# Gates in four parts, block copies in two, and the symmetrised rows of a triangular solve in four strips

## The chip, the cores and the metric

The kernel runs on one core of a Trainium2 chip. The metric is the device time of one execution in microseconds. The kernel before was timed in three runs: 1096.52, 1096.67 and 1097.42 us, a median of 1096.67 us.

Names of engines in the profile: PE is TensorE (matmuls), PEld its weight loads, DVE is VectorE, ACT is ScalarE, POOL is GpSimd, SP is the engine that issues the DMAs here.

## The reference

One layer of a hybrid model on 384 tokens of 1024 channels: 128 context tokens, which start from zero states and use their own conditioning vector, and 256 latent tokens, which start from cached states. The same weights serve both.

```python
x += 0.5 * gate1 * swiglu_1(rmsnorm(x) * (1 + scale1) + shift1)
P  = (rmsnorm(x) * (1 + scale2) + shift2) @ w_in          # 1024 -> 9248
yA = W_a(B * conv3(C * x_a))                              # short gated convolution
yB = W_dn(rmsnorm_head(o_fwd + o_bwd) * silu(z))          # two-way gated DeltaNet, 8 heads of 128
x += gate2 * W_o(sigmoid(g_A) * yA + sigmoid(g_B) * yB)
x += 0.5 * gate3 * swiglu_2(rmsnorm(x) * (1 + scale3) + shift3)
y  = rmsnorm(x)
```

For the DeltaNet, `g = -exp(a_log) * softplus(a_raw + dt_bias)` is a decay for each token, head and direction; chunks of tokens build `T = I + tril(beta * (k k^T) * decay, -1)` and solve a unit triangular system with it. The matrix `T` depends on the keys and gates alone, so it is inverted once for each head, direction and chunk. The outputs are the normalised tokens and the new forward and backward states.

## The kernel before

**Layout and matmuls.** Channels lie on partitions, the 384 tokens along the free axis, as three blocks of 128. Every large product is made in split fp32: a weight unit of 128 × 1024 numbers, loaded by DMA, is rounded by ACT into a high part `hi` (L270), DVE subtracts to get the low part `lo` (L280), and three matmuls of 384 columns (L288, L289, L290: high × high, high × activations' low part, low × high) are accumulated for each of the unit's eight 128 × 128 blocks. So a unit is 24 matmuls, in two **halves** of 12. The third matmul of a unit is the first that reads `lo`. Both parts are made for the unit after next: `hi` is issued behind the first half of a unit, `lo` behind the second.

**Order of the work.** Each engine runs its instructions in the order in which the program writes them. All small work (convolutions, gates, the DeltaNet) is written as Python generators, which the function `gemm` moves forward between its halves by two calls, `tick("V")` and `tick("P")`: each calls every live generator once, if it is in that phase. A pair `yield; yield` in a generator means "go on one half later"; what stands between two such pairs is issued in one piece, on whatever engines it uses. The order of the generators in a gap is: queued evacuations, the DeltaNet, the gates, other evacuations.

**Gates.** `gates` (L655 to L727) makes the decays. It transposes the raw gate columns (`nat`), runs exponentials on ACT (L682, L683), evaluates the softplus by a polynomial of 17 small DVE instructions in one piece (L695 to L710), waits `GLAG[3]` = 4 halves beside a pair of its own, sums the decays with matmuls into `cs`, and exponentiates them into `ex`. The exact sums of `g` are also used by the decay masks of the DeltaNet (L836 to L853).

**Evacuations.** `evac_qkv` takes each head's q, k or v from PSUM: ACT copies it into a padded tile (L797, edges L756 and L757) and makes the middle tap of the convolution (L761), one half later DVE adds the outer taps (L766, L767), one half later again ACT makes a tanh `ct` (L808) and DVE the SiLU `kT`, `qT` or `cy` (L810), some yields later PE transposes the result (L815).

**DeltaNet.** `dn` (L858 to L1224) runs once for each group of four heads; the second group starts when the first sets `free`. It builds the masked matrices `M` (L914), copies their 32 × 32 diagonal blocks into `Md` (L940 to L947: eight copies for two directions, half of them on ACT at L945, half on DVE at L947), all in one gap; one half later DVE transposes the blocks (L951, `Lt`) and adds the transpose (L953) to get the symmetrised rows `L3`, 1024 elements on each partition, and one tick later the solve starts: 31 columns (L996 to L1008), each a product (L1000) and a subtraction (L1002) over `(j+1)·n` elements, where `n = 31 - j`. A running `cost` decides how many columns share a gap: when it exceeds `LCOST[gr]` the generator yields, lets another generator (`fst`, matmuls with the cached states) take a step, and yields again. Summed by that formula, the solve of group 0 (0.7) is cut at 25 places and the one of group 1 (0.9) at 19. After the solve stand two transposes (L1010, L1012) and eight block copies (`diag`, L1027 on ACT and L1029 on DVE), all issued in one piece. The inverse is then completed by matmuls and the outputs normalised (a power on POOL at L1210, L1213 on DVE, twelve scalings on ACT at L1219).

**What runs beside it.** While group 0 is in the solve, PE runs the units of w_in that feed the short convolution (its evacuations are L1314 and L1326). Three pairs of units for the gate and output convolution (`pairs_(0, NP0)`, L1356) stand before the loop at L1357, which would tick without matmuls until `free` is set. Then the k, q and v heads of group 1 and the remaining pairs (evacuation L1347) run beside the second group.

Of the kernel before, what the change touches and what calls it, by code (L numbers as in the profile page):

```python
# [9 lines left out]
ALU = mybir.AluOpType  # L10
# [8 lines left out]
FB = 22  # L19
H = 8  # L20
EPS = 1e-6
LCOST = (0.7, 0.9)
NP0 = 3
LAG = (7, 5, 9)
GLAG = (2, 2, 0, 4)
K1 = 2
NMM = 3
R1 = 4
# [123 lines left out]
def program(nc, tc, a, o, ctx, ExitStack):  # L152
    V, A, G, T = nc.vector, nc.scalar, nc.gpsimd, nc.tensor
    LEFT, RIGHT = "left", "right"

    def bc(ap, *shape):
        return ap.to_broadcast(list(shape))
# [27 lines left out]
    def sbank(name="sd"):  # L185
        return pss.tile([P, 512], F32, tag="sd", name=name)
# [394 lines left out]
    def residual(x, k, out, gates):  # L581
        for c, s0, s1 in SEG:
            V.scalar_tensor_tensor(x[:, k, s0:s1], out[:, s0:s1], gates[:, k, c:c + 1], x[:, k, s0:s1],  # L583
                                   op0=ALU.mult, op1=ALU.add)
# [70 lines left out]
    def gates(hf, wba, gp, tmp, res):  # L655
        def lag(n):
            for _ in range(2 * n):
                yield
        yield from lag(GLAG[0])
        pba = sbank("pba")  # L660
        for k in range(8):
            g = k % 4
            T.matmul(pba[32 * g:32 * g + 32, :NT], wba[:, k, :], hf[:, k, :], start=(k < 4), stop=(k >= 4))
        res["pba"] = pba
        yield
        ba = tmp()
        A.activation(ba, pba[:, :NT], AF.Copy)
        na = gp.tile([P, 16], F32, name="na")
        A.activation(na, W["alog"], AF.Exp)
        V.tensor_scalar(na, na, -1.0, None, op0=ALU.mult)  # L670
        yield
        yield from lag(GLAG[1])
        nat = sbank("nat")
        for b in range(3):
            T.transpose(nat[:, b * P:(b + 1) * P], ba[:, b * P:(b + 1) * P], C["ident"])
        yield
        nv = ba[:, :96].rearrange("p (b c) -> p b c", b=3)
        q, x, e, s, s2, s4, p = (ba[:, i:i + 48] for i in (0, 96, 144, 192, 240, 288, 336))
        V.tensor_reduce(nv, nat[:, :NT].rearrange("p (b g c) -> p b c g", b=3, g=4), axis=AX.X, op=ALU.add)
        V.tensor_tensor(x.rearrange("p (b c) -> p b c", b=3), nv[:, :, 16:32], bc(W["dtb"].unsqueeze(1), P, 3, 16),  # L680
                        op=ALU.add)
        A.activation(e, x, AF.Abs)  # L682
        A.activation(e, e, AF.Exp, scale=-1.0)  # L683
        beta = gp.tile([P, 2, 3, 8], F32, name="beta")
        g = gp.tile([P, 2, 3, 8], F32, name="g")
        A.activation(beta, nv[:, :, 0:16].rearrange("p b (d h) -> p d b h", d=2), AF.Tanh, scale=0.5)
        G.tensor_scalar(beta, beta, 0.5, 0.5, op0=ALU.mult, op1=ALU.add)
        nab = bc(na.unsqueeze(1), P, 3, 16)

        def b16(t):  # L690
            return t.rearrange("p (b c) -> p b c", b=3)
        yield
        yield
        yield from lag(GLAG[2])
        V.tensor_scalar(s, e, 2.0, None, op0=ALU.add)  # L695
        V.reciprocal(s, s)
        V.tensor_tensor(s, s, e, op=ALU.mult)
        V.tensor_tensor(s2, s, s, op=ALU.mult)
        V.scalar_tensor_tensor(b16(x), b16(x), 0.0, nab, op0=ALU.max, op1=ALU.mult)
        V.tensor_tensor(s4, s2, s2, op=ALU.mult)  # L700
        V.scalar_tensor_tensor(b16(s), b16(s), 2.0, nab, op0=ALU.mult, op1=ALU.mult)
        V.tensor_scalar(p, s4, 1.0 / 13, None, op0=ALU.mult)
        V.tensor_scalar(q, s4, 1.0 / 15, None, op0=ALU.mult)
        for n in (9, 5):
            V.scalar_tensor_tensor(p, p, 1.0 / n, s4, op0=ALU.add, op1=ALU.mult)
            V.scalar_tensor_tensor(q, q, 1.0 / (n + 2), s4, op0=ALU.add, op1=ALU.mult)
        V.scalar_tensor_tensor(q, q, 1.0 / 3, s2, op0=ALU.add, op1=ALU.mult)
        V.scalar_tensor_tensor(p, p, 1.0, q, op0=ALU.add, op1=ALU.add)
        V.tensor_tensor(p, p, s, op=ALU.mult)
        V.tensor_tensor(g, p.rearrange("p (b d h) -> p d b h", b=3, d=2),  # L710
                        x.rearrange("p (b d h) -> p d b h", b=3, d=2), op=ALU.add)
        yield
        yield from lag(GLAG[3])
        cs = sbank("cs")
        g2 = g.rearrange("p d b h -> p d (b h)")
        for j, masks in enumerate(((C["le"], C["ge"]), (strict[:, 0].bitcast(F32), strict[:, 1].bitcast(F32)))):
            for d in range(2):
                T.matmul(cs[:, j * 48 + 24 * d:j * 48 + 24 * d + 24], masks[d], g2[:, d], start=True, stop=True)
        T.matmul(cs[:, 96:144], ones, g.rearrange("p d b h -> p (d b h)"), start=True, stop=True)
        yield  # L720
        ex = gp.tile([P, 3, 2, 3, 8], F32, name="ex")
        A.activation(ex.rearrange("p a d b h -> p (a d b h)"), cs[:, :144], AF.Exp)
        gh = gp.tile([P, 2, 3, 8], F32R, name="gh")
        gl = gp.tile([P, 2, 3, 8], F32, name="gl")
        A.activation(gh, g, AF.Copy)
        V.tensor_tensor(gl, g, gh.bitcast(F32), op=ALU.subtract)
        res["beta"], res["gs"], res["ex"] = beta, (gh.bitcast(F32), gl), ex  # L727


    def mixer(x, acc, esb, es, nt, raw, tail_pool, on_wo):  # L730
# [127 lines left out]
        def dn(gr, d, dp, ready):  # L858
# [38 lines left out]
            for b in range(3):  # L897
# [3 lines left out]
                if b == 0:  # L901
                    V.tensor_scalar(n2, d["ssk"], 4.0 * EPS, None, op0=ALU.add)
                    G.tensor_tensor(rk.rearrange("p b h -> p (b h)"), n2.rearrange("p b h -> p (b h)"), phalf[:, :12],
                                    op=ALU.pow)
# [18 lines left out]
            def scores():  # L923

                while not ready("q", 4):
                    yield
                V.tensor_scalar(nq, d["ssq"], 4.0 * EPS, None, op0=ALU.add)
                G.tensor_tensor(rq.rearrange("p b h -> p (b h)"), nq.rearrange("p b h -> p (b h)"), mhalf[:, :12],
                                op=ALU.pow)
                for b in range(3):  # L930
                    kq = sbank("kq")
                    four(kq, lambda h: kT[:, h, b * P:(b + 1) * P], lambda h: qT[:, h, b * P:(b + 1) * P])
                    yield
                    for dd in range(2):
                        V.tensor_tensor(f2(Dm[dd][:, b]), kq, f2(Dm[dd][:, b]), op=ALU.mult)
                    yield
                V.tensor_scalar(rq, rq, float(P) ** -0.5, None, op0=ALU.mult)
            post = scores()

            for dd in range(2):  # L940
                for q in range(4):
                    src = Mn[dd][32 * q:32 * q + 32, :, 32 * q:32 * q + 32]
                    dst = Md[32 * q:32 * q + 32, :, 12 * dd:12 * dd + 12].rearrange("p i n -> p n i")
                    if q % 2 == 0:
                        A.activation(dst, src, AF.Copy)  # L945
                    else:
                        V.tensor_copy(dst, src)  # L947
            yield
            yield
            Lt = dp.tile([P, 32, 32], F32, tag="Lt", name="Lt")  # L950
            V.transpose(Lt, Md)  # L951
            L3 = dp.tile([P, 32, 32], F32, tag="Md", name="L3")
            V.tensor_tensor(L3, Lt, Lt.rearrange("p i j -> p j i"), op=ALU.add)  # L953
            Z3 = Zl
            yield
            egc, edec, egl = (ex[:, i, :, :, h0:h0 + 4] for i in range(3))
# [38 lines left out]
            cost = 0.0  # L995
            for j in range(31):  # L996
                n = 31 - j
                t = dp.tile([P, 256], F32, tag="lt", name="lt")
                t3 = t[:, :(j + 1) * n].rearrange("p (c i) -> p c i", i=n)
                V.tensor_tensor(t3, bc(Z3[:, 0:j + 1, j:j + 1], P, j + 1, n),  # L1000
                                bc(L3[:, j:j + 1, j + 1:32], P, j + 1, n), op=ALU.mult)
                V.tensor_tensor(Z3[:, 0:j + 1, j + 1:32], Z3[:, 0:j + 1, j + 1:32], t3, op=ALU.subtract)  # L1002
                cost += 0.4 + 2.1e-3 * (j + 1) * n
                if cost > LCOST[gr] and j < 30:
                    cost = 0.0
                    yield
                    next(fst, None)
                    yield  # L1008
# [280 lines left out]
        def start(gr):  # L1289
            d = holder["d"]  # L1290
            while "ex" not in res:
                yield
                yield
            spawn(dn_decay(gr, d, dp), now=False)
            yield from dn(gr, d, dp, lambda kinds, n: all(nev.get(k, 0) >= 4 * gr + n for k in kinds))

        gen = spawn(start(0), now=False)
        spawn(gates(hf, wba, gp, lambda: t384("cv"), res), "P", now=False)

        ch = cpl.tile([P, 8, NT], F32R, tag="c0", name="ch")  # L1300
# [443 lines left out]
```

## Time and profile before

| | |
|---|---|
| median of three runs | 1096.67 us |
| the profiled execution | 1097.54 us |
| its span | 1095.8 us |
| mean granted clock of TensorE | 0.994 |
| PE busy | 1076.1 us (98%) |
| DVE busy | 796.7 us (73%) |
| ACT busy | 485.3 us (44%) |
| POOL busy | 119.2 us (11%) |
| gates' polynomial, L695 to L710 | 354.32 to 357.54 us |
| block copies, `Lt` and `L3` of group 0 (DVE) | 2.11, 1.24 and 2.08 us |
| solve of group 0, first column | at 415.76 us |
| solve of group 1, first and last column | at 596.96 and 639.97 us |

A row of a timeline reads: start, duration, engine, line, operation, output <- inputs, partitions × elements, and in brackets the idle time before it and what ended it. Neighbouring instructions of one kind are joined (xN). A row of a table of stretches has, for each engine, the busy time and the count, then the TensorE clock that was granted (1.00 is full speed), the DMA share and the traffic. A row of waits has the total, the number and the longest.

### The profile page before, as it was taken

What the parts mean: (1) busy time and instruction counts of PE and PEld (TensorE: products, weight loads), DVE (VectorE), ACT (ScalarE), POOL (GpSimd) and SP (SyncE); (2) the same over time, 40 slices, a digit from 0 to 9 for tenths busy, and PEclk for the clock granted to TensorE, in tenths of its full rate; (3) what the DMA queues carried; (4) which work ended last, traced back from release to release, by engine and by line L of the source; (5) the groups of instructions that cost most, each with busy time, mean ns of one, the idle gap of its engine ahead of it and who ended that gap; (6) DMA issues with size and microseconds to landing.
All of it is one profiled execution on the core that took longest, in us unless ns stands there. A gap on an engine that the chain in (4) does not pass through costs nothing. (4 is left out here: it accounts for less than half of the span.)

```text
span 1095.8 us, 17468 instructions
## 1 busy us (share of the span) xinstructions
PE 1076.1 (98%) x7031; PEld 1056.8 (96%) x7031; DVE 796.7 (73%) x1367; ACT 485.3 (44%) x907; POOL 119.2 (11%) x102
## 2 busy tenths in 40 slices
PE   9999999999999999999999999999999999999997
PEld 7799999999998999999998999999999999999997
DVE  3799988898879899985599986555669765443442
ACT  3563333322357873352586343343357333333332
POOL 1300000000031441011360111100011000000000
PEclk9999999999999999999999999999999999999999
DMA  9566756666435423332332432336425643333331
GB/s 367 203 244 247 269 209 249 233 233 253 147 121 173 135 78 102 129 116 83 131 109 85 128 132 78 126 115 230 143 89 206 220 182 122 115 131 125 118 128 58
DMA packets 35969, 174.34 MB, mean 159 GB/s; under 512 B 3376, under 2 KB 10288, under 8 KB 22704
## 3 DMA queue, kind: packets, MB, share of 16 engines
q1 hardware_dynamic: 35888, 173.23, 44.3%
q8 instruction: 55, 0.90, 0.3%
q14 instruction: 26, 0.21, 0.1%
HBM read 166.66 MB, written 6.55 MB: 158 GB/s over the span
## 5 line engine op out<-in xcount | busy, mean ns | idle before, releaser
L288 PE MATMUL mm<-hh,hi 128*128 128x384 f32 x1200 | 406.9, 339 | 0.0
L290 PE MATMUL mm<-hh,lo 128*128 128x384 f32 x1200 | 402.7, 336 | 2.3 <-DVE lo L280 2.1
L289 PE MATMUL mm<-hl,hi 128*128 128x384 f32 x1200 | 402.1, 335 | 0.0
L270 ACT ACTIVATE hi<-raw 128x1024 fp32r<-128x1024 f32 (+1 forms) x238 | 242.0, 1019 | 274.3 <-PE mm L289 177.2
L280 DVE TENSOR_TENSOR lo<-raw,hi 128x1024 fp32r<-128x1024 f32 (+1 forms) x238 | 286.0, 1203 | 100.0 <-ACT hi L270 99.8
L290 PEld LDWEIGHTS mm<-hh,lo 128*128 128x128 f32 x1200 | 225.8, 188 | 3.8 <-DVE lo L280 3.8
L288 PEld LDWEIGHTS mm<-hh,hi 128*128 128x128 f32 x1200 | 226.0, 188 | 1.5 <-issue 0.6
L289 PEld LDWEIGHTS mm<-hl,hi 128*128 128x128 f32 x1200 | 225.9, 188 | 0.6 <-DVE hl L555 0.2
L481 DVE SCALAR_TENSOR_TENSOR junk<-adw,cb 128x1024 f32<-128x1024 f32 x112 | 136.6, 1219 | 0.7
L288 PE MATMUL mm<-ah,hi 128*128 128x384 f32 x352 | 117.6, 334 | 0.0
L289 PE MATMUL mm<-al,hi 128*128 128x384 f32 x352 | 117.6, 334 | 0.0
L290 PE MATMUL mm<-ah,lo 128*128 128x384 f32 x352 | 117.6, 334 | 0.0
L288 PEld LDWEIGHTS mm<-ah,hi 128*128 128x128 f32 x352 | 66.1, 188 | 0.0
L289 PEld LDWEIGHTS mm<-al,hi 128*128 128x128 f32 x352 | 66.1, 188 | 0.0
L290 PEld LDWEIGHTS mm<-ah,lo 128*128 128x128 f32 x352 | 66.1, 188 | 0.0
L618 DVE TENSOR_TENSOR gu<-mm,sg 128x384 f32<-128x384 f32 x38 | 21.2, 557 | 35.6 <-PE mm L290 35.6
L442 DVE TENSOR_TENSOR al<-gu,ah 128x384 fp32r<-128x384 f32 x44 | 24.2, 556 | 17.2 <-ACT ah L441 17.2
L575 ACT ACTIVATE sqt<-xT 128x384 f32<-128x384 f32 x20 | 10.5, 525 | 58.1 <-DVE xT L583 58.1
L552 POOL TENSOR_TENSOR xr<-xT,sqacc 128x384 f32<-128x384 f32 x24 | 29.3, 1233 | 28.9 <-DVE h L566 9.7
L746 POOL MEMSET xp<- 128x396 f32 x3 | 1.2, 429 | 251.4 <-DVE al L442 161.0
L1634 POOL TENSOR_TENSOR r<-ms,mhalf 128x1 f32<-128x1 f32 x1 | 0.5, 548 | 255.2 <-DVE ms L1633 255.2
L331 DVE SCALAR_TENSOR_TENSOR xl<-xT,amod,xh 128x128 fp32r<-128x128 f32 (+1 forms) x48 | 27.3, 605 | 1.2 <-ACT xh L321 1.1
(326 smaller groups left out, 1369.3 us busy)
## 6 DMA issues: line engine op xcount, KB each, us to landing
raw<-wts SPq DMA_DIRECT2D x91, 1024.0 KB, 4.9
adw<-adaT SPq DMA_DIRECT2D x28, 1024.0 KB, 7.1
raw<-wts SPq DMA_DIRECT2D x16, 896.0 KB, 4.6
ad<-ada SPq DMA_DIRECT2D x8, 1024.0 KB, 10.5
raw<-wts SPq DMA_DIRECT2D x10, 768.0 KB, 4.4
cb<-condb SPq DMA_DIRECT2D x2, 1024.0 KB, 7.6
raw<-wts SPq DMA_DIRECT2D x4, 384.0 KB, 9.7
xsp<-xT SPq DMA_DIRECT2D x1, 1536.0 KB, 9.7
```

The lines of the kernel that those rows point to most:

```text
L270: A.activation(hi[:, :n], raw, AF.Copy)
L280: V.tensor_tensor(lo[:, :n], raws[c][:, off:off + n], hi[:, :n].bitcast(F32), op=ALU.subtract)
L288: T.matmul(out, wh[:, off:off + width], rh, start=first, stop=False)
L289: T.matmul(out, wh[:, off:off + width], rl, start=False, stop=False)
L290: T.matmul(out, wl[:, off:off + width], rh, start=False, stop=last)
L331: V.scalar_tensor_tensor(xl[:, s0:s1], x[:, k, s0:s1], amod[:, i, k, c:c + 1], xh[:, s0:s1].bitcast(F32), op0=ALU.mult, op1=ALU.subtract)
L442: V.tensor_tensor(lo, x, hi.bitcast(F32), op=ALU.subtract)
L481: V.scalar_tensor_tensor(junk, t[:, s], 1.0, cb[:, c], op0=ALU.mult, op1=ALU.mult, accum_out=modT[:, v, j + s, c:c + 1])
L552: G.tensor_tensor(xs[k], x[:, k, :], rbs, op=ALU.mult)
L575: A.activation(t, x[:, k, :], AF.Square)
L618: V.tensor_tensor(t, pu, sg, op=ALU.mult)
L746: G.memset(t, 0.0)
```

## The change

Four edits, no matmul or DMA is added or removed.

1. The polynomial of the gates is cut into four parts of 4, 5, 4 and 4 instructions, each one half after the part before; `GLAG[3]` goes from 4 to 2.
2. The block copies of the two directions stand in two gaps, one half apart, and begin one half later than before.
3. The add that makes `L3` is cut into four strips of eight rows; each is written ahead of the column that first needs it (0, 8, 16, 24) and only from the strip's second column on: 8 × 31, 8 × 23, 8 × 15 and 8 × 7 elements instead of 1024. The running cost is raised by 0.003·n at each.
4. `LCOST` goes from (0.7, 0.9) to (0.8, 1.0). By the formula the solve of group 0 is then cut at 23 places, the one of group 1 at 15.

```diff
-LCOST = (0.7, 0.9)
+LCOST = (0.8, 1.0)
...
-GLAG = (2, 2, 0, 4)
+GLAG = (2, 2, 0, 2)
...
         V.tensor_tensor(s2, s, s, op=ALU.mult)
+        yield
+        yield
         V.scalar_tensor_tensor(b16(x), b16(x), 0.0, nab, op0=ALU.max, op1=ALU.mult)
...
         V.tensor_scalar(q, s4, 1.0 / 15, None, op0=ALU.mult)
+        yield
+        yield
         for n in (9, 5):
             V.scalar_tensor_tensor(p, p, 1.0 / n, s4, op0=ALU.add, op1=ALU.mult)
             V.scalar_tensor_tensor(q, q, 1.0 / (n + 2), s4, op0=ALU.add, op1=ALU.mult)
+        yield
+        yield
         V.scalar_tensor_tensor(q, q, 1.0 / 3, s2, op0=ALU.add, op1=ALU.mult)
...
             post = scores()
 
+            yield
+            yield
             for dd in range(2):
                 for q in range(4):
...
                     else:
                         V.tensor_copy(dst, src)
-            yield
-            yield
+                yield
+                yield
             Lt = dp.tile([P, 32, 32], F32, tag="Lt", name="Lt")
             V.transpose(Lt, Md)
             L3 = dp.tile([P, 32, 32], F32, tag="Md", name="L3")
-            V.tensor_tensor(L3, Lt, Lt.rearrange("p i j -> p j i"), op=ALU.add)
...
             for j in range(31):
                 n = 31 - j
+                if j % 8 == 0:
+                    V.tensor_tensor(L3[:, j:j + 8, j + 1:32], Lt[:, j:j + 8, j + 1:32],
+                                    Lt[:, j + 1:32, j:j + 8].rearrange("p i j -> p j i"), op=ALU.add)
+                    cost += 0.3e-2 * n
```

## The prediction

> **What bounds the kernel now.** I read the page's busy shares first, then the whole list of waits on TensorE, then each of those waits in the timelines of PE, DVE and ACT.
>
> ```profile
> span 1095.8 us, 17468 instructions
> PE 1076.1 (98%) x7031; PEld 1056.8 (96%) x7031; DVE 796.7 (73%) x1367; ACT 485.3 (44%) x907; POOL 119.2 (11%) x102
> PE mm L290 <- DVE lo L280: 5.2, 4, 2.5
> PE tr L815 <- DVE kT L810: 2.9, 1, 2.9
> ```
>
> TensorE sets the time. It is busy for 1076.1 of 1095.8 us, and in the stretch that the change touches it waits five times: once for `kT` (2.9 us) and four times for the low half of a weight unit, `lo` (5.2 us together). No matmul is added or removed, so the change is worth what it does to these five waits, to the clock after them, and to waits that do not exist yet. The five in PE's timeline:
>
> ```profile
> 354.85 0.34 PE L290 MATMUL mm<-hh,lo 128*128 128x384 f32 x1
> 358.07 0.55 PE L815 MATMUL tr<-cst,kT 128*128 128x128 f32 x3 [2.88 <-DVE kT L810]
> ...
> 418.17 0.34 PE L289 MATMUL mm<-hl,hi 128*128 128x384 f32 x1
> 420.23 0.44 PE L290 MATMUL mm<-hh,lo 128*128 128x384 f32 x1 [1.72 <-DVE lo L280]
> ...
> 543.40 0.44 PE L290 MATMUL mm<-hh,lo 128*128 128x384 f32 x1 [0.41 <-DVE lo L280]
> ...
> 597.79 0.34 PE L289 MATMUL mm<-cl,hi 128*128 128x384 f32 x1
> 600.60 0.45 PE L290 MATMUL mm<-ch,lo 128*128 128x384 f32 x1 [2.48 <-DVE lo L280]
> ...
> 612.01 0.44 PE L290 MATMUL mm<-ch,lo 128*128 128x384 f32 x1 [0.56 <-DVE lo L280]
> ```
>
> Successive matmuls start about 0.17 us apart when nothing stops them, so each wait costs its start-to-start gap less 0.17: 3.05 at 358, 1.89 at 420, about 0.58 at 543, 2.64 at 600.6 and about 0.73 at 612. After two of them the granted clock falls. Columns of the next rows: stretch, length, then busy time and count for PE, PEld, DVE, ACT, POOL, then the granted clock.
>
> ```profile
> 358.07:362.09 4.02, 4.02 (x16) 4.02 (x16) 3.40 (x5) 3.50 (x19) 0.00 (x0) 0.58 0.48 145
> 600.60:604.60 4.00, 4.00 (x15) 3.90 (x16) 3.76 (x11) 2.23 (x4) 0.00 (x0) 0.57 0.74 250
> 569.00:646.00 77.00, 73.97 (x448) 73.10 (x447) 73.70 (x155) 38.23 (x87) 6.76 (x6) 0.98 0.33 109
> ```
>
> At clocks of 0.58 and 0.57 these stretches lose 0.42 × 4.02 = 1.69 and 0.43 × 4.00 = 1.72 us. The last row matters most: over the 77 us of head group 1's preparation and solve, DVE is busy for 73.70. There DVE, not PE, sets the pace.
>
> **The change part by part.** First the gates.
>
> ```profile
> 354.32 0.22 DVE L695 TENSOR_SCALAR cv<-cv 128x48 f32<-128x48 f32 x1
> 355.30 0.21 DVE L698 TENSOR_TENSOR cv<-cv 128x48 f32<-128x48 f32 x1
> 357.33 0.21 DVE L710 TENSOR_TENSOR g<-cv 128x48 f32<-128x48 f32 x1
> 357.46 0.55 DVE L810 SCALAR_TENSOR_TENSOR kT<-ct,cy 128x384 f32<-128x384 f32 x1
> 356.03 0.51 ACT L808 ACTIVATE ct<-cy 128x384 f32<-128x384 f32 x1
> ```
>
> The polynomial's 17 instructions hold DVE from 354.32 to 357.46, and `kT`, which PE transposes next, stands behind them. In four parts only L695 to L698 stay ahead of it, and they end near 355.5. But `kT` also needs `ct` from ACT, whose row ends at 356.54. So `kT` runs 356.6 to 357.15 instead of 357.46 to 358.0, and the transpose starts near 357.2: 0.9 us saved, not 3.05. The other three parts take (357.46 − 355.42) = 2.0 us in later half units; they fit into DVE's waits for `ct`. Without that cover one of them delays a `lo` by at most 0.9 (the largest part). A second gain hangs on the clock: the idle time shrinks from 2.88 to about 2.0, between 1.72 (after which the profile shows no dip) and 2.48 (after which it does). If the dip goes, 1.69 more is saved. I take a dip as 35% likely: 0.9 + 0.65 × 1.69 = **−2.0**; ends −2.6 and 0 (a part in the way of a `lo`). The shorter GLAG nets to one half unit (12 matmuls, 12 × 0.173 = 2.08 us) later for the decay sums and all of group 0 behind them.
>
> [...]
>
> Now head group 0's solve.
>
> ```profile
> 412.01 1.24 DVE L951 STREAM_TRANSPOSE Lt<-Md 128x1024 f32<-128x1024 f32 x1
> 413.28 2.08 DVE L953 TENSOR_TENSOR L<-Lt 128x1024 f32<-128x1024 f32 x1
> 418.95 1.22 DVE L280 TENSOR_TENSOR lo<-raw,hi 128x1024 fp32r<-128x1024 f32 x1
> ```
>
> The wait at 420.23 is for the `lo` at 418.95, behind which stand 1.24 + 2.08 us of one-off work and the 2.11 us of block copies. The change deals the copies into two gaps and the add into strips of 8 × 31, 8 × 23, 8 × 15 and 8 × 7 = 608 of 1024 elements. At the row's 2.08 us per 1024, with 0.17 fixed for each (the shortest rows of the solve, 31 elements, take 0.17 to 0.19), the strips take 4 × 0.17 + 608 × 1.87 ns = 1.81 us, the first 0.63. Rows of plain L1000 products of the same sizes (0.41 for 247 elements, down to 0.22 for 60) would make it 1.3. So it saves 0.27 to 0.8 in all, and 1.45 ahead of column 0. With two halves (4.16 us) more room for copies and transpose, and 1.45 less in the way, the `lo` that was 1.89 late has some 4 us to spare. The wait of 1.89 and a tail of about 0.3 at 426 go: −2.2. The other side: LCOST 0.8 packs the columns of this group into 23 half-unit pairs of ticks instead of 25 (counted by summing 0.4 + 2.1e-3·(j+1)·n, plus 0.3e-2·n at each strip, against the bound), so the middle gaps hold more and one `lo` near 438 comes about 0.7 late. **−1.5**; ends −2.2 and 0.
>
> Group 0's end then comes one half unit later in program order (+1 gates, +2 copies, −2 columns) while it is the same work.
>
> ```profile
> 537.51 3.63 ACT L1219 ACTIVATE on<-on,mo 128x128 f32<-128x128 f32 x12 [5.92 <-DVE mo L1213]
> 542.12 2.36 DVE L280 TENSOR_TENSOR lo<-raw,hi 128x1024 fp32r<-128x1024 f32 x2 [4.71 <-ACT hi L270]
> ```
>
> ACT's twelve L1219 instructions hold up `hi`, `hi` holds up `lo`, and PE loses 0.58 at 543. Moved a half later the same block stands before the first `kT` of group 1 as well; I price that as one more wait of the same size: **+0.5**; ends 0 (it lands where ACT has room) and +1.0 (two more).
>
> Then group 1, where the sign of the whole is decided.
>
> ```profile
> 586.66 3.67 ACT L945 ACTIVATE Md<-M 32x384 f32<-32x384 f32 x4
> 590.35 0.52 ACT L808 ACTIVATE ct<-cy 128x384 f32<-128x384 f32 x1
> 590.90 0.56 DVE L810 SCALAR_TENSOR_TENSOR cy<-ct,cy 128x384 f32<-128x384 f32 x1 [1.09 <-ACT ct L808]
> 593.79 2.07 DVE L953 TENSOR_TENSOR L<-Lt 128x1024 f32<-128x1024 f32 x1
> 599.33 1.22 DVE L280 TENSOR_TENSOR lo<-raw,hi 128x1024 fp32r<-128x1024 f32 x1
> ...
> 636.84 1.22 DVE L280 TENSOR_TENSOR lo<-raw,hi 128x1024 fp32r<-128x1024 f32 x1
> 640.00 1.25 DVE L1010 STREAM_TRANSPOSE O<-Zl 128x1024 f32<-128x1024 f32 x1
> 645.57 1.23 DVE L280 TENSOR_TENSOR lo<-raw,hi 128x1024 fp32r<-128x1024 f32 x1
> ...
> 641.92 0.34 PE L290 MATMUL mm<-ch,lo 128*128 128x384 f32 x1
> 646.98 0.34 PE L290 MATMUL mm<-hh,lo 128*128 128x384 f32 x1
> ```
>
> The wait at 600.6 vanishes where it is: strips and an earlier transpose bring its `lo` forward by 2 to 4 us, and it needs 2.64. But PE then only runs into a queue that has not become shorter. The `lo` that starts at 645.57 ends at 646.80 and its matmul starts at 646.98: after 2.64 + 0.73 + 1.72 = 5.1 us of lost PE time, DVE is just on time. Take away the early wait and the same 5.1 us come back later unless DVE's work shrinks or moves. Four things move it. The strips save 0.27 to 0.8. The one idle time of DVE, 1.09 at 590.9, becomes about 2.4, since ACT's copies (3.67 us for four) are dealt into two gaps and the second pair stands ahead of the `ct` that DVE needs, while less DVE work covers it: +1.3. LCOST 1.0 packs 31 columns into 15 half-unit pairs instead of 19; with the copies' +2 the closing block (L1010 to the last L1029, 640.00 to 645.57) moves two halves, one unit, ahead in program order. So the block must now be done before the `lo` of the unit before, whose matmul stands at 641.92. The new time of that `lo` is the old block's end, 645.57, less the 1.7 us of the old `lo` and the L1347 merge behind it that now come later, plus 1.3 idle, less 0.5 strips, plus 1.2 for itself: about 645.9; bounds 644.6 (no new idle) to 646.4. PE reaches it at 641.92 plus one `kq` of 0.8 us that moves ahead too: 642.7. That is 1.9 to 3.7 more of wait than now; **I take +2.5**, as a little of it falls where the clock is down anyway. Ends: −5.1 (DVE is not the limit after all and the waits simply go) and +5.0 (3.3 plus one more dip of 1.7 behind the last wait).
>
> Sum: −2.0 − 1.5 + 0.5 + 2.5 = **−0.5**. The profiled execution took 1097.54, 0.87 above the median of 1096.67, so 1097.54 − 0.5 − 0.87 = **1096.2 us**.
>
> [...]
>
> **Rivals.** *Faster, group 1's waits break even or go.* For it: PE's idle time of 2.48 and its dip stand at one place, and the change takes the work away from that place; a DVE share of 73.70 in 77.00 still leaves 3.3 us. Against it: the matmul at 646.98 with nothing to spare. If group 1 breaks even, −2.0 − 1.5 + 0.5 = −3.0, 1093.7; if its waits go altogether, −8.1, 1088.6. *Slower, the packed solve of group 1 drops the clock behind its last wait.* Fifteen gaps hold what nineteen held, the closing block stands a unit earlier, and PE waits there in one piece for up to 3.7 us; from some 2.5 us of idle time the clock falls, and at the end of the stage nothing is left that a slower PE could wait for, so 1.7 counts in full: group 1 costs +5.0. With the dip at 358 kept as well (−0.9 there) the sum is −0.9 − 1.5 + 0.5 + 5.0 = +3.1, 1099.8. Against it: the waits may split into short ones, as at 600 and 612 now. *The polynomial's split does nothing*, since `ct` sets `kT`'s start: that alone moves the sum by +0.9 and stays within what can be told apart.
>
> **How the numbers follow.** About 0.2%, 2.2 us, is what a measurement of this kernel can tell from no change. My forecast (−0.5, reaching ±2.2) has 0.40. Group 1 breaking even or better has 0.36, of which 0.12 for its waits going altogether. The slower rival has 0.24. Range: 1089.0 to 1100.3, which leaves out the fullest form of either side; the forecast's own range is 1094.5 to 1098.9. Faster 0.36, same 0.40, slower 0.24.
>
> **What would show it.** Stall 1: the `kT` wait at 355 shorter than 2.88 and naming `ct` behind it, and whether the clock is 1.00 from 358 to 362. Group 0: no `lo` wait near 420, a shorter one near 438. Group 0's end: L1219, `hi` and `lo` around 543 to 550. Group 1: the 600.6 wait gone and new `lo` waits between 605 and 647, DVE's share from 569 to 646 above 0.95 with an idle time at `ct` near 590, and O1 a unit earlier against PE. I am wrong if the sum of `lo` waits in group 1 falls below 3 us with O1 moved ahead: then DVE was not the limit.

## The result, and the profile after

The change makes the kernel slower: 1103.19 us in the median (1101.34 to 1104.3), against 1097.05 us for the kernel before timed beside it, a ratio of 1.0062 (95% interval 1.0050 to 1.0074), or some 6 us. The forecast was 1096.2 with a range up to 1100.3. The profiled execution of the changed kernel took 1101.34 us, so it is the quickest of its four, 1.9 us below their median.

Its page, and the whole list of waits on TensorE in the stretch from 300 to 720 us:

```profile
span 1099.6 us, 17474 instructions
PE 1074.4 (98%) x7031; PEld 1053.3 (96%) x7031; DVE 796.8 (72%) x1373; ACT 483.7 (44%) x907; POOL 120.7 (11%) x102
PE mm L290 <- DVE lo L280: 10.4, 8, 3.0
PE tr L821 <- DVE kT L816: 2.6, 3, 2.0
```

PE's work is what it was, and so is DVE's (796.8 against 796.7). The waits for `kT` are shorter, as forecast, but those for `lo` have doubled, from 5.2 to 10.4 us. (Line numbers move by 6 behind the gates and by 11 from the solve on: L810 is L816, L1000 is L1011.) PE's timeline has them at these places:

```profile
355.46 0.55 PE L821 MATMUL tr<-cst,kT 128*128 128x128 f32 x3 [1.99 <-DVE kT L816]
...
421.67 0.44 PE L290 MATMUL mm<-hh,lo 128*128 128x384 f32 x1 [0.91 <-DVE lo L280]
...
432.31 0.44 PE L290 MATMUL mm<-hh,lo 128*128 128x384 f32 x1 [0.26 <-DVE lo L280]
...
437.47 0.44 PE L290 MATMUL mm<-hh,lo 128*128 128x384 f32 x1 [0.73 <-DVE lo L280]
...
479.08 0.44 PE L290 MATMUL mm<-hh,lo 128*128 128x384 f32 x1 [1.52 <-DVE lo L280]
...
603.08 0.44 PE L290 MATMUL mm<-hh,lo 128*128 128x384 f32 x1 [1.16 <-DVE lo L280]
608.53 0.44 PE L290 MATMUL mm<-ch,lo 128*128 128x384 f32 x1 [0.66 <-DVE lo L280]
616.28 0.44 PE L290 MATMUL mm<-hh,lo 128*128 128x384 f32 x1 [2.98 <-DVE lo L280]
...
646.53 0.44 PE L290 MATMUL mm<-ch,lo 128*128 128x384 f32 x1 [2.21 <-DVE lo L280]
```

To see where time comes from and goes to, I matched the mixer's main matmuls of the two traces in their order and took the difference of their starts, at places where no small PE work stands on different sides. The first is at 333.94 before and 332.23 after. That difference of 1.71 us is older than any changed instruction, so it is taken off.

| same matmul, before | after | after less before, less the start | what lies in the stretch |
|---|---|---|---|
| 333.94 | 332.23 | 0 | |
| 367.71 | 363.49 | −2.51 | gates: shorter wait, no dip of the clock |
| 457.27 | 453.89 | −1.67 | rest of the gates' delay, most of group 0's solve |
| 534.16 | 533.14 | +0.69 | closing block of group 0 |
| 573.65 | 572.95 | +1.01 | group 0's output, first keys of group 1 |
| 741.53 | 745.31 | +5.49 | all of group 1 |

So 2.5 us are won at the gates, 3.5 are lost again by the end of group 0, and 4.5 in group 1. The sum of 5.5 is close to the 6 us of the medians. From here on "by 457", "by 574" and "by 742" mean these differences at the third, fifth and sixth place.

**Group 0's solve.** DVE's rows ahead of the `lo` that PE waits for at 421.67 and, last, POOL's:

```profile
416.61 0.64 DVE L1006 TENSOR_TENSOR L<-Lt 128x248 f32<-128x248 f32 x1
417.28 0.92 DVE L1011 TENSOR_TENSOR lt<-Zl,L 128x31 f32<-128x31 f32 x1
418.23 0.97 DVE L1013 TENSOR_TENSOR Zl<-Zl,lt 128x31 f32<-128x31 f32 x1
419.23 0.99 DVE L1011 TENSOR_TENSOR lt<-Zl,L 128x60 f32<-128x60 f32 x1
420.26 0.22 DVE L1013 TENSOR_TENSOR Zl<-Zl,lt 128x60 f32<-128x60 f32 x1
420.40 1.22 DVE L280 TENSOR_TENSOR lo<-raw,hi 128x1024 fp32r<-128x1024 f32 x1
416.61 3.54 POOL L994 TENSOR_TENSOR vn<-vn,rk 128x512 f32<-128x512 f32 x3 [17.62 <-ACT vn L825]
```

While POOL multiplies `vn`, the first three rows of the solve take 0.92 to 0.99 instead of about 0.2 us, 2.2 us more ahead of that `lo`. In the kernel before POOL starts this work at 421.71, behind the wait at 420. The four strips themselves take 0.64, 0.49, 0.38 and 0.25, together 1.76 (forecast 1.81).

**Group 0's closing block.** ACT's rows and one of DVE's, of the changed kernel:

```profile
472.14 1.84 ACT L1038 ACTIVATE XP<-O 32x384 f32<-32x384 f32 x2 [6.81 <-DVE O L1023]
473.99 1.81 ACT L1038 ACTIVATE M<-O 32x384 f32<-32x384 f32 x2
475.83 1.06 ACT L270 ACTIVATE hi<-raw 128x1024 fp32r<-128x1024 f32 x1
476.80 0.51 ACT L441 ACTIVATE ch<-cv 128x384 fp32r<-128x384 f32 x1
477.21 0.47 ACT L1316 ACTIVATE xp<-mm 128x384 f32<-128x384 f32 x1
477.58 1.04 ACT L270 ACTIVATE hi<-raw 128x1024 fp32r<-128x1024 f32 x1
477.81 1.22 DVE L280 TENSOR_TENSOR lo<-raw,hi 128x1024 fp32r<-128x1024 f32 x1
```

Four block copies hold ACT for 3.65 us. Behind them stand `hi` and `ch`, and the `lo` that PE waits for at 479.08 stands on DVE behind the instruction that needs `ch` (L442, which waits 2.78). The kernel before has the same ACT rows at nearly the same times and the same `lo` at 477.85, but there PE comes to the matmul that needs it only at 481.37 and doesn't wait.

**Group 1's packed gap.** DVE's rows and, last, POOL's:

```profile
611.05 0.40 DVE L1011 TENSOR_TENSOR lt<-Zl,L 128x231 f32<-128x231 f32 x1
611.48 1.28 DVE L1013 TENSOR_TENSOR Zl<-Zl,lt 128x231 f32<-128x231 f32 x1
612.80 1.13 DVE L1011 TENSOR_TENSOR lt<-Zl,L 128x240 f32<-128x240 f32 x1
613.97 1.13 DVE L1013 TENSOR_TENSOR Zl<-Zl,lt 128x240 f32<-128x240 f32 x1
615.01 1.21 DVE L280 TENSOR_TENSOR lo<-raw,hi 128x1024 fp32r<-128x1024 f32 x1
611.47 3.36 POOL L994 TENSOR_TENSOR vn<-vn,rk 128x512 f32<-128x512 f32 x3 [36.88 <-DVE lt L1011]
```

While POOL multiplies `vn`, three column instructions take 1.28, 1.13 and 1.13 instead of about 0.4 us: 2.3 us more for DVE, in a gap that holds a strip and four columns ahead of the `lo` at 615.01. PE waits 2.98 for it, and the granted clock falls to 0.69 in the next 4 us; behind the later wait at 646.5 it stays at 1.00:

```profile
616.00:620.00 4.00, 3.72 (x15) 3.72 (x16) 3.76 (x10) 0.00 (x0) 0.00 (x0) 0.69 0.00 0
...
646.00:650.00 4.00, 3.47 (x20) 3.47 (x21) 4.00 (x8) 2.95 (x4) 2.27 (x1) 1.00 0.62 162
...
569.00:646.00 77.00, 70.51 (x427) 69.07 (x425) 72.92 (x156) 37.62 (x91) 7.00 (x7) 0.98 0.29 95
```

**Group 1's closing block.** The last of these rows shows DVE busy for 72.92 of 77 us, nearly as before (73.70); PE has fallen from 73.97 to 70.51. DVE's first closing transpose begins at 639.74 (640.00 before) and the `lo` behind the block at 645.25 (645.57 before), but it is now the `lo` of a unit earlier:

```profile
594.86 0.56 DVE L816 SCALAR_TENSOR_TENSOR cy<-ct,cy 128x384 f32<-128x384 f32 x1 [1.63 <-ACT ct L814]
...
639.74 1.25 DVE L1021 STREAM_TRANSPOSE O<-Zl 128x1024 f32<-128x1024 f32 x1
...
645.25 1.23 DVE L280 TENSOR_TENSOR lo<-raw,hi 128x1024 fp32r<-128x1024 f32 x1
```

### The profile page after: what moved, and what is told of

The parts are those of the page before. It is cut to its first block, busy times and chain, and to the rows that moved or that the text cites. A ratio compares the mean times of both kernels' runs of the same rounds, so it can differ in the third digit from the quotient of the medians.

```text
span 1099.6 us, 17474 instructions
## 1 busy us (share of the span) xinstructions
PE 1074.4 (98%) x7031; PEld 1053.3 (96%) x7031; DVE 796.8 (72%) x1373; ACT 483.7 (44%) x907; POOL 120.7 (11%) x102
## 5 line engine op out<-in xcount | busy, mean ns | idle before, releaser
L442 DVE TENSOR_TENSOR al<-gu,ah 128x384 fp32r<-128x384 f32 x44 | 24.2, 556 | 17.3 <-ACT ah L441 17.3
```

The lines of the kernel that those rows point to most:

```text
L442: V.tensor_tensor(lo, x, hi.bitcast(F32), op=ALU.subtract)
```

## The experiments

All kernels compute the same outputs; none leaves work out. In the tables a ratio is to the kernel before on the same chip (its median was 1095.0 to 1095.7 us there, and 1097.05 for the row of the changed kernel), and "by ..." is from one profile each. A profile is one execution and can lie off its kernel's median: those of `l_g0` and the changed kernel are 2.9 and 1.9 us quicker than it, those of `g_only` and `cs_v` 2.4 slower. So a "by ..." says where time goes in that execution, and the ratio says what the edit costs.

### Each edit alone

The four parts of the diff, one at a time: `g_only` the gates with GLAG 2, `c_only` the copies, `s_only` the strips, `l_only` the bounds:

```diff
-LCOST = (0.7, 0.9)
+LCOST = (0.8, 1.0)
```

> Before with the gates edit alone (polynomial in four parts, GLAG 2). Theory P (the loss comes from packing the solve of group 1 into 15 gaps): the transpose wait at 358 falls from 2.88 to 2.0 us, no clock dip after it, 2 us gained there, of which the closing block of group 0 (near 470 to 480) may take back up to 1; in all 1095 to 1096.5, group 1 as before. Rival C (the split block copies cost): the same here. Rival S (what is gained before a solve is always lost in it, since DVE sets its end): 1097, the 2 us come back as lo waits between 415 and 480.

> Before with the copies edit alone (a gap earlier for nothing, one direction in each of two gaps). Theory P: group 1's block comes two halves later against PE, so DVE has 4 us more room: its lo waits fall by 2 to 4 us, 1093.5 to 1096. Rival C: DVE's idle time for ct grows from 1.1 to 1.6 us or more and the solve begins later: 1098 to 1100. Rival S: 1097 within 1.

> Before with the strips alone (LCOST as before; the first group then is cut at 25 places, the second at 20 since the strips count). Theory P: 0.3 to 0.8 us less DVE work for each group and 1.4 less ahead of the first column, one cut more in group 1: 1094 to 1096.5. Rival C: the same. Rival S: 1096 within 1, as only DVE's own saving counts.

> Before with LCOST (0.8, 1.0) alone: the first solve cut at 23 places instead of 25, the second at 14 instead of 19. Theory P: the closing block of group 1 stands 5 halves (10 us of matmuls) earlier, lo waits there grow by 4 us or more: 1100 to 1106. Rival C: no loss, since the copies are as before: 1096 to 1098. Rival S: DVE's work is the same, so its end in time is the same and the total moves by less than 1.5.

| kernel | median us | ratio (95%) | by 457 | by 574 | by 742 |
|---|---|---|---|---|---|
| changed kernel | 1103.19 | 1.0062 (1.0050 to 1.0074) | −1.67 | +1.01 | +5.49 |
| g_only | 1098.49 | 1.0029 (1.0019 to 1.0040) | +1.19 | +3.23 | +3.47 |
| c_only | 1095.01 | 0.9992 (0.9983 to 1.0001) | −2.02 | −0.85 | −0.73 |
| s_only | 1099.66 | 1.0031 (1.0019 to 1.0044) | −1.62 | −1.59 | +3.14 |
| l_only | 1107.51 | 1.0115 (1.0098 to 1.0133) | −0.25 | +2.45 | +9.76 |

The bounds alone cost 12 us, twice as much as the whole change: the copies and strips make up for part of it. In `l_only` the second solve is cut at 14 places, and its `lo` waits are 3.6 and 2.7 us, each followed by a clock of about 0.5.

The gates alone, on which my sum rested for its largest gain, lose 0.3%. Their transposes wait 2.0 instead of 2.88 as forecast, but then DVE, whose chain of decay masks now stands half a unit later, is met by a PE that is 2.5 us further.

```profile
420.18 0.69 PE L290 MATMUL mm<-hh,lo 128*128 128x384 f32 x1 [3.95 <-DVE lo L280]
...
420.00:424.50 4.50, 4.32 (x16) 4.32 (x17) 4.33 (x10) 2.23 (x4) 2.84 (x3) 0.62 0.00 0
```

Some of the 3.95 is chance: in this profile, the slowest of the seven executions, POOL's decay masks have delayed DVE's chain in the way that the section "Which bound" shows for `l_g1`, where it was worth 1.2 us. At the next closing block PE waits 1.51 (at 482.95), as in the changed kernel.

The copies alone take away the wait at 420 altogether, −2.0, and give 1.1 us back as a wait for the first `kT` of group 1. In group 1 they gain nothing: two halves more room for its end don't help while the wait at 600 stays (2.62, with a dip to 0.50), and the idle time at `ct` grew to 1.6.

The strips alone shorten both solves: −1.6 by 574, and −3.4 at the matmul at 650.7 of the kernel before, behind group 1's block, as they should. Then 2.49 us are lost in one piece at a place where nothing signals a releaser (the last section comes back to it), with a dip behind it (0.50), and some 1.1 in two waits at the output transposes (below, the first of them):

```profile
661.99 0.39 PE L288 MATMUL mm<-hh,hi 128*128 128x384 f32 x1 [2.49 <-issue]
...
713.43 0.30 PE L1419 MATMUL otr<-cst,on 128*128 128x128 f32 x1 [0.63 <-DVE on L1219]
```

Theory P (packing group 1's solve) and rival S each hold in part: S for the gates, P for the bounds. Rival C falls: the copies don't cost. In time P was right for the copies alone; `g_only`, `s_only` and `l_only` came out slower than all their ranges.

### Pairs, and the gates at their old half

`cs` is copies and strips; `no_g` and `no_l` are the changed kernel without its gates edit and without its bounds; `g1` is the gates alone with one lag less:

```diff
-GLAG = (2, 2, 0, 4)
+GLAG = (2, 2, 0, 1)
```

> Copies and strips, gates and LCOST as before (cuts 25 and 20). Theory Q (each edit's gain or loss hangs on where its group's DVE work then stands against the units, and LCOST's fewer cuts are what costs): no lo wait in group 0 (copies alone had none), group 1's first wait falls from 2.6 below 1.0 with no dip as with the strips alone: 1090 to 1094 unless the late code load of the strips kernel near 660 comes again (+4). Rival E (edits don't add: every half later at group 1's end costs at its output transposes near 713): 1096 to 1099.

> The changed kernel without its gates edit: copies, strips, LCOST (0.8, 1.0); cuts 23 and 15. Theory Q: group 0 gains 2 as with the copies alone, group 1 loses as in the changed kernel (block a unit earlier, +4.5): 1097 to 1101. Rival G (the gates edit is what spoils the changed kernel, as it cost 3.3 us alone): 1093 to 1096.

> The changed kernel with LCOST as before (0.7, 0.9): gates, copies, strips; cuts 25 and 20. Theory Q: group 1 is given back its room, its lo waits fall from 7.0 to below 3 us: 1092 to 1097. Rival G: no better than 1099, since the gates' half unit stays.

> Gates edit with GLAG[3] 1 instead of 2, all else as before: the decay sums, and all of group 0 behind them, stand at the same half as before. Theory Q: the transposes' wait is 2.0 without a dip (-2.5), and the lo wait near 420 is 2 to 4 without the extra half, so that at most half the gain is lost: 1094 to 1096. Rival S (DVE sets the end of group 0's solve whatever the half): as with GLAG 2, a wait of about 4 us with a dip near 420: 1098 to 1099.

| kernel | median us | ratio (95%) | by 457 | by 574 | by 742 |
|---|---|---|---|---|---|
| cs | 1095.16 | 0.9992 (0.9979 to 1.0004) | −2.41 | −1.19 | −0.39 |
| no_g | 1099.42 | 1.0040 (1.0026 to 1.0054) | −2.18 | −1.28 | +3.72 |
| no_l | 1095.12 | 1.0000 (0.9990 to 1.0011) | −2.59 | −1.36 | −0.43 |
| g1 | 1095.57 | 1.0003 (0.9993 to 1.0012) | −0.84 | −0.91 | −1.06 |

Without the bounds the change costs nothing; without the gates it still costs 0.4%. So LCOST is what makes it slower. The gates edit is harmless once the copies and strips stand beside it under the old bounds (`no_l` 1.0000, `cs` 0.9992); under the new ones it still adds some 0.2%. `cs` was a miss for both theories: at 1095.16 it lies between Q's range and E's. Its first wait in group 1 did fall, to 1.17 without a dip (matmuls 0.17 apart behind it), but 0.66 and 1.50 follow it, and 1.1 at the output transposes. With GLAG 1 the decay sums wait for the polynomial instead (1.25 us), and the gain at the gates is 0.9, not the 2.5 that GLAG 2 had there.

### Which bound

`l_g0` is the changed kernel with LCOST (0.8, 0.9), `l_g1` with (0.7, 1.0). `cs19` is `cs` with the strips not counted in the cost, which cuts the second solve at 19 places instead of 20, and `g1cs19` adds the gates with GLAG 1:

```diff
-                    cost += 0.3e-2 * n
```

> The changed kernel with LCOST (0.8, 0.9): only group 0's bound raised (cuts 23 and 20). Theory Q2 (it is the second bound, 1.0, that costs: 15 cuts pack group 1's solve until DVE is late): group 1 as with the old bounds, 1095 to 1096.5. Rival F (the first bound costs: its closing block falls a unit earlier and waits near 437 and 479 take the gain at the gates away): 1097.5 to 1099.

> The changed kernel with LCOST (0.7, 1.0): only group 1's bound raised (cuts 25 and 15). Theory Q2: lo waits near 616 (3 us, with a dip) and near 646 (2.2) as in the changed kernel: 1099 to 1102. Rival F: 1095 to 1096.5.

> Copies and strips, gates and LCOST as before, and the strips not counted in the cost, so that group 1 is cut at 19 places (the kernel with copies and strips had 20). Theory Q3 (an odd number of halves at group 1's end, not the strips, brings the waits at the output transposes near 713): those waits of 1.3 us vanish as with the copies alone, group 1's first waits stay near 3.3: 1093 to 1094.5. Rival T (whatever shortens the solve brings the end of group 1 to the output transposes late or early by the same amount): as with 20 cuts, 1095.

> The same with the gates edit and GLAG[3] 1 (decay sums at the half of before). Theory Q3: a further 0.9 at the gates, as the gates alone kept with GLAG 1, and nothing lost in group 0: 1092 to 1093.5. Rival T: 1094 to 1095.

| kernel | median us | ratio (95%) | by 457 | by 574 | by 742 |
|---|---|---|---|---|---|
| l_g0 | 1099.73 | 1.0041 (1.0026 to 1.0056) | −1.70 | +0.93 | +1.66 |
| l_g1 | 1100.63 | 1.0054 (1.0038 to 1.0069) | −0.48 | +0.67 | +5.19 |
| cs19 | 1096.45 | 1.0011 (1.0001 to 1.0021) | −2.43 | −1.28 | +2.44 |
| g1cs19 | 1095.37 | 1.0004 (0.9994 to 1.0013) | −3.44 | −2.26 | −0.08 |

Both bounds cost, and not in sum: 0.41 and 0.54% one at a time, 0.62 together. The first costs at group 0's closing block: `l_g0` has the changed kernel's wait of 1.52 at 478.3, `no_l` has none there. That isn't the whole of it: the profiles of the two end 2.1 us apart, the medians some 4.5. The profiled execution of `l_g0` is its quickest (1096.81 at a mean granted clock of 0.997; the other four took 1099.52 to 1101.4 at 0.993 or 0.994), so about half of the first bound's cost is not in the trace, and its place stays open. Its median lies above the ranges of both theories. The second costs in group 1 (+4.5, against +0.9 in `no_l`). `cs19` was a miss: one cut fewer put 2.91 us of wait, with a dip to 0.50, in the place of 1.50 near 613, though the waits at the output transposes went as expected. In it, as in the changed kernel, the late `lo` lies behind instructions that POOL's multiplication stretches. `g1cs19` was a miss for the same reason: 2.98 at 612.6, with a dip to 0.50, takes back more than the 0.9 that it gains at the gates, and its 1095.37 lies above both ranges.

`l_g1` and `no_l` are the same program up to the end of group 0, yet `l_g1` stands 2.1 us worse by 457. DVE's rows of `no_l`, and one of POOL's:

```profile
390.58 0.61 DVE L772 SCALAR_TENSOR_TENSOR cy<-xp,vec,cy 128x384 f32<-128x384 f32 x1
391.22 1.28 DVE L773 SCALAR_TENSOR_TENSOR cy<-xp,vec,cy 128x384 f32<-128x384 f32 x1
...
390.58 1.51 POOL L842 TENSOR_TENSOR gm<-cst,gl 128x512 fp32r<-128x512 f32 x1
```

and of `l_g1`:

```profile
390.49 1.46 DVE L772 SCALAR_TENSOR_TENSOR cy<-xp,vec,cy 128x384 f32<-128x384 f32 x1
391.98 1.53 DVE L773 SCALAR_TENSOR_TENSOR cy<-xp,vec,cy 128x384 f32<-128x384 f32 x1
...
390.49 1.04 POOL L842 TENSOR_TENSOR gm<-cst,gl 128x512 fp32r<-128x512 f32 x1
```

POOL makes decay masks at the same time (`gm` and `Dm`, from 389.5 in both). In both, DVE's first tap and POOL's next mask begin in the same hundredth of a microsecond. In the one execution DVE's tap is untouched and POOL's mask takes 1.51; in the other DVE's takes 1.46 and POOL's 1.04. The same code leaves DVE 1.2 us later by the end of these masks, and PE then waits 2.52 instead of 0.91 for a `lo` near 422, with a dip (0.58 from 422 to 426). The tie comes with the gates at GLAG 2: DVE goes first in the profiles of the changed kernel, `no_l` and `l_g0`, POOL in those of `g_only`, `l_g1`, `after_v`, `no_l_v`, `n19_v` and `n21_v`.

### Taking POOL's multiplication away

The scaling of `vn` moves from three instructions on POOL to twelve on ACT, four in each of three gaps:

```diff
-                for bb in (1, 2, 0):
-                    G.tensor_tensor(vn[:, bb], vn[:, bb], bc(rk[:, bb].unsqueeze(2), P, 4, P), op=ALU.mult)
+                for h in range(4):
+                    A.activation(vn[:, bb, h], vn[:, bb, h], AF.Copy, scale=rk[:, bb, h:h + 1])
```

> The changed kernel with GpSimd's three multiplications of vn (L994) made as twelve scalings on ScalarE, four in each of three gaps. Theory X (the collision of GpSimd with DVE makes the packed gaps late): no DVE column of 1.1 us is left, the wait near 616 falls from 3.0 to below 1.0 without a dip, the one near 421 goes; 1097 to 1099. Rival P (the packing by itself): the waits stay within 0.5 of what they were, 1101 to 1104.

> The kernel before with the same move to ScalarE. Theory X: the collision there falls behind the last late lo of group 1 (615 to 618), and in group 0 behind the wait at 420, so little is gained: 0 to 2 us, 1094 to 1096. Rival P: no gain or a loss of up to 1 from ScalarE's twelve instructions ahead of hi.

> Gates, copies and strips with LCOST as before (equal to the kernel before) and vn on ScalarE. Theory X: the waits of 0.9 near 421 and 1.5 near 612 go: 1091.5 to 1093.5. Rival P: 1094.5 to 1096.

> Copies and strips alone with vn on ScalarE. Theory X: the wait of 1.5 near 613 goes, group 0 had none: 1092 to 1094. Rival P: 1095 to 1096.

| kernel | median us | ratio (95%) | by 457 | by 574 | by 742 |
|---|---|---|---|---|---|
| after_v (changed kernel) | 1099.97 | 1.0042 (1.0026 to 1.0058) | −2.74 | −0.13 | +3.59 |
| b_v (kernel before) | 1094.93 | 1.0000 (0.9991 to 1.0010) | −0.41 | −0.43 | −0.49 |
| no_l_v | 1093.78 | 0.9980 (0.9971 to 0.9989) | −3.61 | −2.39 | −3.37 |
| cs_v | 1093.16 | 0.9980 (0.9971 to 0.9989) | −2.39 | −1.19 | −2.11 |

In `after_v` the wait at 616 falls from 2.98 to 0.63 and no dip follows (matmuls start 0.17 apart): that wait was the collision. But most of the loss stays and shows where it had been hidden:

```profile
613.38 0.44 PE L290 MATMUL mm<-hh,lo 128*128 128x384 f32 x1 [0.63 <-DVE lo L280]
...
635.42 0.44 PE L290 MATMUL mm<-hh,lo 128*128 128x384 f32 x1 [0.63 <-DVE lo L280]
643.59 0.44 PE L290 MATMUL mm<-ch,lo 128*128 128x384 f32 x1 [2.82 <-DVE lo L280]
```

The closing block's wait grows from 2.21 to 2.82, now with a dip to 0.50: DVE's whole queue up to that block is longer than what PE has to do until then, and removing a wait ahead of it only makes PE come sooner. So of group 1's +4.5 the collision itself is worth 0.8 (+3.7 is left), and the two rivals are both right in their part: X for the wait at 616, P in that most of the loss stays. The median, 1099.97, lies between their ranges. In group 0 the wait at 421 falls from 0.91 to 0.28, and the kernel stands at −2.74 by 457 instead of −1.67. Where the closing block has its room (`no_l`, `cs`) the same move wins 2.2 and 1.3 us by the ratios (`no_l_v` came out 0.3 above X's range, `cs_v` within it). In the kernel before it wins nothing, since there the collision, from 614.97 on, falls behind the last late `lo` (612.01).

### A version that beats both

`n19_v` and `n21_v` are gates (GLAG 2), copies, strips (not counted in the cost) and `vn` on ACT, with 19 and 21 cuts in group 1 (LCOST (0.7, 0.9) and (0.7, 0.85)).

> Gates, copies and strips, LCOST (0.7, 0.9) with the strips not counted (19 cuts in group 1), vn on ScalarE. Theory O (an odd number of halves brings the waits of the output transposes): those 1.3 us go, no wait near 612 since the collision is gone: 1091.5 to 1093. Rival N (the number of cuts, whatever its parity): the waits stay, or the closing block's lo wait comes back: 1093.5 to 1095.

> The same with 21 cuts in group 1 (bound 0.85). Theory O: even as well, the same 1091.5 to 1093. Rival N: later still at the output transposes, 1094 to 1097.

| kernel | median us | ratio (95%) | by 457 | by 574 | by 742 |
|---|---|---|---|---|---|
| n19_v | 1091.28 | 0.9956 (0.9943 to 0.9970) | −3.60 | −2.44 | −3.77 |
| n21_v | 1090.36 | 0.9945 (0.9933 to 0.9958) | −3.66 | −2.50 | −5.31 |

Both are faster than either kernel, the second by 5.2 us, and faster than both ranges of their expectations. Its waits on TensorE from 340 to 720 us:

```profile
PE tr L821 <- DVE kT L816: 3.3, 3, 2.0
PE mm L290 <- DVE lo L280: 2.5, 4, 1.2
```

No `lo` wait reaches 1.3 us, and none comes behind 605. The waits at the output transposes are gone with 19 and 21 cuts; with 20 they were there in all kernels with the copies. That they hang on the odd number of halves fits these rows, but `l_only` (14 cuts, five halves earlier) has no such wait, so it isn't shown as a rule.

## Why the prediction was wrong, step by step

**What bounds the kernel** was read rightly: PE's work didn't change, and the time moved by waits and dips alone.

**The gates' wait** came out as worked out: `ct` sets `kT`, 1.99 us are left of 2.88, no dip follows (1.00 from 355.46 to 360), −2.5 where I took −2.0 between the two cases.

**Group 0's solve**, forecast at −1.5, is the first step that failed, and in it the sentence that the `lo` would have "some 4 us to spare". It counted the copies' two halves and the strips, and these do take the wait away (`c_only`, `cs`: −2.0 and −2.4 by 457). It left out three things. The gates let PE arrive 2.5 us sooner, and they put DVE's chain half a unit later (stated in the step on the gates, but not counted here); alone that makes a wait of 3.95, part of it chance. And POOL's multiplication, which stood behind the late `lo`, now stands ahead of it and costs DVE 2.2 us: without it the change stands at −2.74 by 457 (`after_v`). Together, 0.91, 0.26 and 0.73 us of wait are left, and from the gates to 457 the change loses 0.8 in the table's rows instead of winning 1.5. The wait of 0.7 near 438 was forecast, at its size (0.73 at 437.47).

**Group 0's end**, forecast at +0.5, cost +2.7 from 457 to 574. I looked for it at the twelve scalings near 540; it lies at the closing block near 478. The step named the block copies only for group 1. With the gates and copies in place LCOST 0.8, which moves that block a unit ahead in program order, brings it: `l_g0` has the wait, `no_l` hasn't. The bound by itself doesn't: `g_only`, with the old one, has the same wait, and `l_only`, with the new one, has no `lo` wait there. The four kernels that wait 1.51 to 1.53 at this block (`g_only`, the changed kernel, `l_g0`, `after_v`) are those whose group 0 stands one half later than before, the "+1 gates, +2 copies, −2 columns" that the prediction counted and priced at another place; the five where it stands three halves later wait nothing there.

**Group 1**, forecast at +2.5 and measured at +4.5, had the mechanism right and its size wrong. DVE's share from 569 to 646 was 0.947 (forecast above 0.95), the idle time at `ct` 1.63 (forecast 2.4), the closing `lo` ended at 646.48 (forecast 645.9; with the 1.71 us that this execution is early from the start it is 648.2, 2.3 later than forecast, of which 1.0 was brought along from group 0), and the early wait at 600 went, only to come back behind it. The term that was missed is POOL's multiplication: 2.3 us of stretched columns fall into the fullest gap, where PE waits 2.98 and the clock dips. The trace before had such rows at another place, where they cost nothing, and the prediction left them out.

**The rivals.** The one on the slower side, +3.1 and 1099.8, was nearest and said why: the packed second solve. Its point of decision was wrong: the clock fell behind the wait at 616, not behind the last one, and the dip at 358 wasn't kept. The rival that group 1 breaks even is what the change does with the old bounds (`no_l`: +0.9 there).

The sum missed by 6.0 us: 2.3 in group 0's solve, 2.2 at its end and 2.0 in group 1, less the 0.5 that the gates gave beyond the forecast. In group 0 it was wrong because its terms were added as if each wait stood alone. −2.0 at the gates and −1.5 in the solve are for the most part one and the same slack, which PE can use only where DVE's queue has room: by 457 the copies and strips give −2.41 alone (`cs`) and −2.59 together with the gates (`no_l`).

## What to carry to other kernels

Here a wait removed early was worth something only where the queue behind it was short enough to let the faster engine through (2.51 us won at the gates had become 0.69 lost by 534); follow the gain to the next place where that queue sets the pace before adding it up. When work is packed into fewer gaps, count for each gap what stands ahead of its most urgent instruction, and what another engine does to these instructions' durations at that moment, for the same row may be harmless at one place and decide at another (here POOL's multiplication cost PE nothing at 421.71 and 614.97 in the kernel before, and 2.3 us of DVE's time ahead of a wait of 2.98 in the changed one). Tune the packing last: here the bounds that the change came with cost 7 us, and with others the same edits win 5 once one collision is gone.

## What the runs showed of the hardware

**POOL and DVE in each other's way.** In the profiles of the kernel before and the changed kernel, a DVE instruction that starts while one of POOL's three multiplications of `vn` runs takes 0.72 to 0.88 us more whatever its size (12 rows): 0.17 became 0.92 for 31 elements (417.28, changed kernel), 0.40 became 1.13 for 240 (612.80), 0.56 became 1.40 for 384 (421.81, kernel before). In all of them DVE's row ends behind POOL's, by its own usual time less 0.13 to 0.15: the row of 1.13 at 612.80, which usually takes 0.40, ends 0.26 behind the POOL row that it overlaps. So in these rows DVE does its work when POOL has finished. The six POOL rows take 1.04 to 1.55. Beside POOL's decay masks the same is seen of `lo`: 2.06 instead of 1.22 at 382.81 in the changed kernel, while the mask that starts at 383.76 takes 2.02. Where both start at nearly the same time either can be the one that gives way: at 416.61 in the changed kernel DVE's row takes its usual 0.64 and POOL's 1.55; at 611.47 POOL's takes 1.04 and DVE's, which starts 0.01 later, 1.28 instead of 0.40. With the multiplication on ACT PE's wait behind such rows, 2.98 in the changed kernel, is 0.63 (`after_v`). Every stretched row reads two inputs from SBUF, while L920, which reads one of its two from PSUM, takes 1.12 for four both beside POOL's mask (changed kernel, 389.87) and without it (399.97). Which of the two gives way in such a tie can differ between executions of the same code, as the masks of `no_l` (1.51 on POOL) and `l_g1` (1.46 on DVE) show.

**The clock after a wait.** In the profiles of this study's kernels, none of the 24 PE waits of 1.5 to 2.21 us between 340 and 720 us was followed by a lower clock (1.00 behind each), and 23 of the 27 of 2.32 to 3.95 us were, at 0.50 to 0.57 over 2.5 us. The same wait of 2.9 us at the transposes cost a dip in eight of the nine kernels that have it. The shortest wait with a dip behind it is the 2.32 of `no_g` at 644.74, and four longer ones (2.45 in `g1`, 2.86 and 2.98 in `l_g1`, 2.91 in `l_only`) had none. A dip is worth some 1.6 us: from the start of the transposes to the matmul at 367.71 of the kernel before, `l_only`, whose profile has no dip there, takes 8.08 us and the eight kernels that have one 9.62 to 9.65. So chance of this kind moves a kernel with several such waits from run to run: `l_g0` took 1096.81 us at a mean clock of 0.997 and 1099.5 to 1101.4 at 0.993 or 0.994. It isn't all of the scatter: the four times of the changed kernel, 1101.34 to 1104.3, don't follow their clocks (0.995, 0.996, 0.995, 0.994 from the quickest to the slowest).

**A stall without a releaser.** In `s_only` PE stood still for 2.49 us ahead of 661.99 and in `l_only` for 1.77 ahead of 484.03, in or shortly behind a burst of small matmuls and weight loads (the one at 657.16 in the kernel before has 288 within 1.4 us), with no releaser in the profile; `cs19` has the same in small (0.29 ahead of 661.97). The page lists a queue q8 of the kind "instruction" with 55 packets and 0.90 MB, and in the kernel before PE starts 254 matmuls and weight loads between two of its packets, in the mean. In `s_only` one of these packets ran from 659.72 to 660.64, and the stall ended 1.35 us behind it. That PE had run out of loaded code there, as the expectation of `cs` has it, fits these rows, but it is my reading and isn't shown: the same burst cost the kernel before nothing, and no run changed the loading.
